# A three-block network on one core: more warming matmuls, rounded sums of squares, stacked decay terms, and another closing scaling

## Chip, cores and metric

The kernel runs on one core of one Trainium2 chip. Its time is device microseconds of one launch. The core has TensorE (PE in the rows: matmuls), VectorE (DVE), ScalarE (ACT), GpSimd (POOL) and SyncE (SP, which issues most DMAs). Each engine works through its own queue in order, and an instruction waits at the head of its queue until the semaphores of what it reads have come.

## What is computed

512 tokens of 1024 channels pass through two layers and a second block; every product is followed to float32 accuracy. Cut to what the change touches:

```python
def rms_norm(x, g):                                   # 11 places, all but one over 1024 channels or 256 of a head
    return x * rsqrt(mean(x * x, axis=-1) + EPS) * g

x = x + rglru_mixer(rms_norm(x, g_mix0)); x = x + sq_relu_mlp(rms_norm(x, g_mlp0))      # layer 0
x = x + dsa_mixer(rms_norm(x, g_mix1));   x = x + sq_relu_mlp(rms_norm(x, g_mlp1))      # layer 1
#   dsa_mixer: c = rms_norm(c, kv_norm_g) of the 128 latent channels; top-k keys by index scores; 16 heads
x = rms_norm(x, final_norm_g)                         # end of the first block ...
h = rms_norm(x, norm_mix)                             # ... and at once the first norm of the second
q, k, v, r, lr_f, lr_b, u, g_a, g_b = split(h @ w_in)
log_a_f = log_sigmoid(lr_f @ w_decay_up_fwd + b) / 16 # lr: 16 channels in each direction, decays: 512 in each
log_a_b = log_sigmoid(lr_b @ w_decay_up_bwd + b) / 16
o = gla(q, k, v, log_a_f) + gla reversed(log_a_b)     # 4 heads, o normed over 256 channels per head
x = x + merged(o, pool(u), g_a, g_b) @ w_out;  x = x + (silu(gate) * up) @ w_ffn_out
return rms_norm(x, norm_final)
```

## The kernel before

**Layout.** Activations lie channels on partitions, tokens along the row: eight tiles `xs` of 128x512. A weight chunk (128x1024, the 8 channel tiles of one output tile) is loaded by SyncE three chunks ahead, rounded by ScalarE (`wh`, L246), and GpSimd takes the exact remainder (`wl`, L247). Activations are split the same way, `split` (L350 to 355): `h` by ScalarE, L353, then `l` by VectorE, L354. Rounded numbers have the type fp32r. `group` (L339 to 342) makes a product of three passes over TensorE: wh by xh, wh by xl, wl by xh. An output tile is 24 such passes (`ps`).

**Norms.** `Feed` (L376) scales and splits the residual as it becomes ready and sums its squares tile by tile in `acc`. The norm's factor is applied behind the product: `feed.r`, asked for the first time by the evacuation of the next stage's first output tile, emits `total(acc)` (L365), one product of float32 `ones` with the sum, so that all 128 partitions hold it, and then `rsqrt_mean` (L370 to 373): square root with its table on ScalarE (`std`, L372) and reciprocal on VectorE (L373). `total` is called twelve times: for mix0, mlp0, mix1, mlp1, ffn2, the latent in `c_job` (`csq`), four GLA heads, and twice in `Feed2` (class at L980), which serves the two norms that follow one another with `acc1` and `acc`; its factor takes two reciprocals and four more steps (L993 to 1003).

**Decays.** `lr_job` evacuates the 32 low-rank channels (`lr`, L1034; the output tile holds one direction in rows 0 to 15 and the other in 32 to 47) and splits it. `decay_job`, eight times, multiplies it with one 128-column stretch of `dec`: three passes each.

**Order.** Jobs are lists of stages, and `run` (L262) emits stage n of a job n jobs behind its first; a planning scheduler then orders each engine's queue (ScalarE's by hand in the start). Before the first product of 72 passes on three output tiles (`first_products`, L511), `WARM` bfloat16 products of 128x512 run on a zero tile (L333, 334). In that start VectorE also works through a softplus of 128x8 (`sp`, L475 to 493).

**The end.** The last ffn products are made by halves of the tokens (`last_job`). `tail` norms a half: two products of `ones` with `acc2[0]` (channel tiles 0 to 6) and `acc2[1]` (tile 7), L1421, root L1425, reciprocal L1426, then `outs`: for each of 8 tiles of 128x256 either VectorE's x times gain times factor (L1435), or, for tiles 2, 3 and 7, which ScalarE has scaled by the gain (L1393), GpSimd's product with the factor (L1433); one DMA for each pair.

Of the kernel before, what the change touches and what calls it, by code (L numbers as in the profile page):

```python
# [29 lines left out]
WARM = 7  # L30
# [3 lines left out]
# the first loads in their order: input tiles, and halves of the weight chunks of the first output tiles  # L34
# [33 lines left out]
def bucket_table():  # L68
    """One-hot columns of the buckets of the distances 255, 254, ..., -127, less the last bucket's."""
    dist = 255 - np.arange(N_DIST)  # L70
    oh = np.zeros((32, DIST_PITCH), np.float32)
    oh[t5_buckets(dist), np.arange(N_DIST)] = 1.0
    oh[31, :N_DIST] -= 1.0
    return oh


def pool_edges():
    """window / count at the first and the last positions of every window."""
# [20 lines left out]
def weight_plan():  # L99
    """The key of every weight chunk in the order of use."""  # L100
# [25 lines left out]
def ktiles(w):  # L126
    """[K, N] -> [128, K / 128 * N], the K tiles side by side."""
    k, n = w.shape
    return w.reshape(k // P, P, n).transpose(1, 0, 2).reshape(P, -1)


def pack_weights(a):
    """The weights as one flat array, chunk after chunk in the order of use."""
# [4 lines left out]
    z16 = np.zeros((D, 16), np.float32)  # L138
    lr = np.concatenate([w_in2[:, 3072:3088], z16, w_in2[:, 3088:3104], np.zeros((D, 80), np.float32)], axis=1)
# [4 lines left out]
    dec[0:16, 0:512] = a["w_decay_up_fwd_2"][0]  # L144
    dec[32:48, 512:1024] = a["w_decay_up_bwd_2"][0]
# [74 lines left out]
class Weights:  # L220
    """Streams the weight chunks and splits each into a rounded part and the exact
    remainder, a number of chunks ahead of their use."""
# [39 lines left out]
def run(jobs):  # L262
    """Emits jobs in a software pipeline: stage n of a job goes out n jobs after its first stage."""
# [9 lines left out]
def build(ctx, tc, xT, wall, par, relb, onehot, edges, out):  # L273
# [50 lines left out]
    V.memset(ones, 1.0)  # L324
    ident = cp.tile([P, P], F32, name="ident")
# [4 lines left out]
    # keeps the tensor engine's clock up while the first loads come in  # L330
# [19 lines left out]
    def split(t):  # L350
        """An SBUF tile as a rounded part and the exact remainder."""
# [13 lines left out]
    def total(acc):  # L365
        ps = PS("tot")
        PE.matmul(ps, ones, acc, start=True, stop=True)
        return ps
# [7 lines left out]
    class Feed:  # L376
        """Residual tiles made ready for the next product: scaled by the norm's gain and
        split, their squares summed. The norm's own factor is applied after the product."""
# [87 lines left out]
    # softplus(-lambda); the recurrence's factors are tanh of half its logarithm, so -4 of it goes into  # L466
    # a sigmoid written as (1 + tanh) / 2
# [32 lines left out]
    def first_products():  # L500
        # the first output tiles together, in the order in which their operands come in
# [100 lines left out]
    # position bias by distance, laid out in DRAM for the diagonal reads  # L602
# [35 lines left out]
    # The queries stand in reverse order within their tiles of 128 up to the product with the values,  # L638
    # which makes the position bias of a tile a read of DRAM with two positive strides.
# [85 lines left out]
    def index_job(i, h):  # L725
        """One head's part of the index scores of query tile i."""
# [100 lines left out]
    # persistent tiles with parts that stay zero: the other head's rows of a query tile, and the  # L827
    # position bias of the keys that are further away than the last bucket's start
# [9 lines left out]
    def queries(pair, j):  # L838
        """Both heads' queries of a pair of query tiles, split, the other head's rows zero."""
# [140 lines left out]
    class Feed2(Feed):  # L980
        """The same through two norms one after the other: the first one's gain stays in the residual."""
# [44 lines left out]
    def lr_job():  # L1026
# [5 lines left out]
        def ev():  # L1032
            t = T(name="lr")
            V.tensor_mul(t, st["ps"], feed.r)  # L1034
            LR.extend(split(t))
# [3 lines left out]
    def u_job(g):  # L1039
# [5 lines left out]
        def pool():  # L1045
            # each half of the tokens with 8 more on both sides, zeros beyond the ends
            window = (2, 4, 8, 16)[g]
            st["w"] = []
            for half in range(2):
# [5 lines left out]
                while True:  # L1055
                    # new[:, i] sums the window of w around position i + lo
# [39 lines left out]
    # decays: running sums of log_sigmoid within chunks of 128, both directions  # L1096
    def decay_job(m, h):
        st = {}

        def mm():  # L1100
            if m == 0 and h == 0:
                dc.extend(W.get("dec"))
            ps = st["ps"] = PS("dec")
            o = m * 512 + h * P
            group(ps, [(dc[0][:, o:o + P], dc[1][:, o:o + P], *LR)])
# [105 lines left out]
    def gla_job(h):  # L1211
# [26 lines left out]
        def states():  # L1238
            # the state that enters each chunk, scaled to the chunk's centre
# [127 lines left out]
    feed = nxt  # L1367
    # the output's tiles by pairs of channel tiles and halves of the tokens; part of them GpSimd finishes
    pooled_out = (2, 3, 7)
    fin = {}  # L1370
    acc2 = [None, None]
# [5 lines left out]
    def final_square(d, c):  # L1377
# [5 lines left out]
        if d == 0:  # L1383
            acc2[0] = sq
        elif d < KD - 1:
            V.tensor_add(acc2[0][:, c], acc2[0][:, c], sq[:, c])
        else:
            acc2[1] = sq
        for c0 in range(c.start, c.stop, 256):
            if (d // 2, c0) not in fin:  # L1390
                fin[d // 2, c0] = T(name="fin")
            if d in pooled_out:
# [116 lines left out]
```

## Time and profile before

| | |
|---|---|
| median of 3 runs | 1916.03 us (1913.93 to 1916.14) |
| span of the profiled execution | 1913.6 us |
| TensorE busy | 1858.6 us (97%) |
| GpSimd busy | 996.1 us |
| VectorE busy | 906.4 us |
| ScalarE busy | 799.0 us |

The profiled execution's own time is not given apart from its span; the span runs from the first to the last instruction of one execution, 2.4 us under the median of the runs. A matmul's duration in the rows is modelled with its pipeline; where matmuls follow one another, the distance of their starts is what each takes from TensorE.

### The profile page before, as it was taken

The page shows a single profiled execution, that of the slowest core. Times are in us where ns is not written, and L with a number is a line of the kernel's source. Part 1 is how long each engine was busy: PE and PEld are TensorE (multiplying, and loading weights), DVE is VectorE, ACT ScalarE, POOL GpSimd, SP SyncE. Part 2 cuts the span into 40 slices and gives each one's busy share as a digit, 9 for nine tenths or more (in the row PEclk, how much of TensorE's full clock was granted, in tenths as well). Part 3 has the DMA queues.
Part 4 walks back from the last instruction along what each step waited for, and adds up shares of the span by engine and source line. Part 5 has one row for each costly group of instructions (what it writes and reads, how often), then busy time and mean ns, then how long its engine had stood idle before and what let it go on. Part 6 is the DMA issues. An engine that isn't in the chain of part 4 may idle for free.

```text
span 1913.6 us, 22395 instructions
## 1 busy us (share of the span) xinstructions
PE 1858.6 (97%) x8704; PEld 1545.4 (81%) x8704; DVE 906.4 (47%) x1170; ACT 799.0 (42%) x1248; POOL 996.1 (52%) x594
## 2 busy tenths in 40 slices
PE   8789999999999989999999999999999999999997
PEld 6567888888887778988888887888888888888886
DVE  7997440143338986543024343534466533133125
ACT  5485441233333697343124445345633333232222
POOL 5466544444563664744444457574355555455453
PEclk9999999999999999999999999999999999999999
DMA  5123222222331220233322332231123323232321
GB/s 189 66 69 99 89 98 99 99 95 93 99 110 67 80 48 18 89 100 99 99 92 96 99 100 80 90 113 61 55 78 109 100 88 101 98 100 88 100 85 58
DMA packets 53961, 172.04 MB, mean 90 GB/s; under 512 B 6288, under 2 KB 12640, under 8 KB 53856
## 3 DMA queue, kind: packets, MB, share of 16 engines
q1 hardware_dynamic: 53712, 170.62, 27.5%
q8 instruction: 68, 1.11, 0.2%
q14 instruction: 37, 0.30, 0.1%
q10 hardware_dynamic: 144, 0.00, 0.0%
HBM read 168.48 MB, written 2.12 MB: 89 GB/s over the span
## 4 chain that ended last, share of the span: by engine, by line
PE 85%; DVE 10%; ACT 3%; issue 1%; DMA 0%; POOL 0%; SPq 0%; DVEq 0%; ACTq 0%; POOLq 0%
PE ps L340 18%; PE ps L341 18%; PE ps L342 18%; PE dn L341 8%; PE dn L342 8%; PE dn L340 8%; ACT probs L889 1%; DVE score L766 1%; DVE xc L530 1%; PE o L1271 1%; DVE top L765 1%; PE ps L511 1%; PE v L1176 1%; PE v L1177 1%; PE v L1178 1%
## 5 line engine op out<-in xcount | busy, mean ns | idle before, releaser
L247 POOL TENSOR_TENSOR wl<-wst,wh 128x1024 fp32r<-128x1024 f32 (+2 forms) x314 | 755.1, 2407 | 734.0 <-ACT wh L246 715.7
L246 ACT ACTIVATE wh<-wst 128x1024 fp32r<-128x1024 f32 (+2 forms) x314 | 327.5, 1045 | 825.3 <-PE ps L341 310.3
L340 PE MATMUL ps<-xh,wh 128*128 128x512 f32 x1376 | 541.6, 394 | 8.7 <-DVE biasrow L619 5.6
L342 PE MATMUL ps<-xh,wl 128*128 128x512 f32 x1376 | 535.6, 390 | 0.0
L341 PE MATMUL ps<-xl,wh 128*128 128x512 f32 x1376 | 535.4, 389 | 0.0
L340 PEld LDWEIGHTS ps<-xh,wh 128*128 128x128 f32 x1376 | 258.8, 188 | 65.7 <-issue 8.0
L341 PEld LDWEIGHTS ps<-xl,wh 128*128 128x128 f32 x1376 | 258.8, 188 | 55.8 <-issue 2.6
L342 PEld LDWEIGHTS ps<-xh,wl 128*128 128x128 f32 x1376 | 258.6, 188 | 53.7
L340 PE MATMUL dn<-h,wh 128*128 128x512 f32 (+1 forms) x712 | 271.9, 382 | 0.0
L341 PE MATMUL dn<-l,wh 128*128 128x512 f32 (+1 forms) x712 | 271.3, 382 | 0.0
L342 PE MATMUL dn<-h,wl 128*128 128x512 f32 (+1 forms) x712 | 271.2, 382 | 0.0
L413 DVE TENSOR_TENSOR x<-x,dn 128x512 f32<-128x512 f32 x48 | 33.0, 687 | 325.3 <-PE dn L342 325.3
L340 PEld LDWEIGHTS dn<-h,wh 128*128 128x128 f32 x712 | 133.8, 188 | 26.1
L341 PEld LDWEIGHTS dn<-l,wh 128*128 128x128 f32 x712 | 133.8, 188 | 25.9
L342 PEld LDWEIGHTS dn<-h,wl 128*128 128x128 f32 x712 | 133.8, 188 | 25.7
L354 DVE TENSOR_TENSOR l<-relu,h 128x512 fp32r<-128x512 f32 x64 | 108.6, 1696 | 91.6 <-ACT h L353 91.6
L340 PE MATMUL ps<-h,wh 128*128 128x512 f32 x232 | 91.4, 400 | 12.7 <-DVE xr L525 11.1
L387 DVE SCALAR_TENSOR_TENSOR xl<-x,params,xh 128x512 fp32r<-128x512 f32 x40 | 86.3, 2161 | 27.7 <-ACT xh L386 27.7
L341 PE MATMUL ps<-l,wh 128*128 128x512 f32 x232 | 91.4, 395 | 1.6 <-DVE l L354 1.6
L342 PE MATMUL ps<-h,wl 128*128 128x512 f32 x232 | 91.1, 394 | 0.0
L444 DVE SCALAR_TENSOR_TENSOR relu<-ps,std 128x512 f32<-128x512 f32 x64 | 44.1, 690 | 86.1 <-PE ps L342 85.9
L354 DVE TENSOR_TENSOR l<-u,h 128x512 fp32r<-128x512 f32 x22 | 43.8, 1992 | 51.2 <-ACT h L353 51.2
(313 smaller groups left out, 2333.0 us busy)
## 6 DMA issues: line engine op xcount, KB each, us to landing
wst<-wall SPq DMA_DIRECT2D x300, 512.0 KB, 3.3
btile<-biasdram SPq DMA_DIRECT2D x32, 128.0 KB, 2.9
wst<-wall SPq DMA_DIRECT2D x8, 384.0 KB, 3.1
x<-xT SPq DMA_DIRECT2D x8, 256.0 KB, 5.6
out_dram<-fin SPq DMA_DIRECT2D x8, 256.0 KB, 2.5
wst<-wall SPq DMA_DIRECT2D x6, 256.0 KB, 5.7
params<-par SPq DMA_DIRECT2D x1, 76.5 KB, 4.9
oh<-onehot SPq DMA_DIRECT2D x1, 48.0 KB, 2.9
```

The lines of the kernel that those rows point to most:

```text
L246: self.nc.scalar.activation(h[:, a:b], st[:, a:b], AF.Copy)
L247: self.nc.gpsimd.tensor_sub(l[:, a:b], st[:, a:b], h[:, a:b].bitcast(F32))
L340: PE.matmul(ps, wh, xh, start=i == 0, stop=False)
L341: PE.matmul(ps, wh, xl, start=False, stop=False)
L342: PE.matmul(ps, wl, xh, start=False, stop=i == n - 1)
L354: V.tensor_sub(l, t, h.bitcast(F32))
L387: stt(l, t, g, h.bitcast(F32), op0=ALU.mult, op1=ALU.subtract)
L413: V.tensor_add(xs[j], xs[j], st["ps"])
L444: stt(t, st["ps"], 0.0, feed.r, op0=ALU.max, op1=ALU.mult)
L511: PE.matmul(first_ps[c], a[:, cols], b, start=left[c] == 3 * KD - 1, stop=left[c] == 0)
L530: stt(c[:, n:], t[:, :S - n], pc(f"conv_w{k}", j), c[:, n:], op0=ALU.mult, op1=ALU.add)
L765: V.max(top, acc[:, :w])
```

## The change

Five things, all visible in the diff below; line numbers behind L343 shift by two to eleven.

1. `WARM` goes from 7 to 17.
2. `total` splits the sum of squares (ScalarE `h`, VectorE `l`) and makes two passes with a rounded `ones_r` in place of one float32 product. All twelve callers get it.
3. The low-rank weights are stored three times (rows 0 to 31, 32 to 63, 64 to 95), the decays' weights likewise. Of the evacuated `lr`, ScalarE rounds the whole tile into `lrz`, and VectorE overwrites rows 32 to 63 with the remainder. Before the first product VectorE copies `wl` of rows 64 to 95 into `wh`. One pass over the stacked rows then holds the three terms. The loads keep their size and number.
4. At the end, ScalarE scales every tile by the gain. The squares of tiles 0 to 6 are split when tile 6 is done, the sum of a half is two rounded passes and one float32 product with tile 7's squares. `outs` is four VectorE products of 128x512 a half; GpSimd does none.
5. Comments are taken out.

```diff
-WARM = 7
+WARM = 17
...
-    lr = np.concatenate([w_in2[:, 3072:3088], z16, w_in2[:, 3088:3104], np.zeros((D, 80), np.float32)], axis=1)
+    lr = np.concatenate([w_in2[:, 3072:3104]] * 3 + [np.zeros((D, 32), np.float32)], axis=1)
...
-    dec[0:16, 0:512] = a["w_decay_up_fwd_2"][0]
-    dec[32:48, 512:1024] = a["w_decay_up_bwd_2"][0]
+    for q in range(0, 96, 32):
+        dec[q:q + 16, 0:512] = a["w_decay_up_fwd_2"][0]
+        dec[q + 16:q + 32, 512:1024] = a["w_decay_up_bwd_2"][0]
...
+    ones_r = cp.tile([P, P], F32R, name="ones_r")
+    V.tensor_copy(ones_r, ones)
...
     def total(acc):
         ps = PS("tot")
-        PE.matmul(ps, ones, acc, start=True, stop=True)
+        h, l = split(acc)
+        PE.matmul(ps, ones_r, h, start=True, stop=False)
+        PE.matmul(ps, ones_r, l, start=False, stop=True)
         return ps
...
-            t = T(name="lr")
+            t, z = T(name="lr"), T(F32R, "lrz")
             V.tensor_mul(t, st["ps"], feed.r)
-            LR.extend(split(t))
+            act(z, t, AF.Copy)
+            V.tensor_sub(z[32:64], t[32:64], z[32:64].bitcast(F32))
+            LR.append(z)
...
-                dc.extend(W.get("dec"))
+                hi, lo = W.get("dec")
+                V.tensor_copy(hi[64:96], lo[64:96].bitcast(F32))
+                dc.append(hi)
             ps = st["ps"] = PS("dec")
             o = m * 512 + h * P
-            group(ps, [(dc[0][:, o:o + P], dc[1][:, o:o + P], *LR)])
+            PE.matmul(ps, dc[0][:, o:o + P], LR[0], start=True, stop=True)
...
-            acc2[0] = sq
+            acc2.append(sq)
         elif d < KD - 1:
             V.tensor_add(acc2[0][:, c], acc2[0][:, c], sq[:, c])
+            if d == KD - 2:
+                h, l = sums[c.start] = T(F32R, "h"), T(F32R, "l")
+                act(h[:, c], acc2[0][:, c], AF.Copy)
+                V.tensor_sub(l[:, c], acc2[0][:, c], h[:, c].bitcast(F32))
         else:
-            acc2[1] = sq
+            last_sq[c.start] = sq
...
-            if d in pooled_out:
-                act(fin_half(d, slice(c0, c0 + 256)), xs[d][:, c0:c0 + 256], AF.Copy, scale=pc("g_fin2", d))
+            act(fin_half(d, slice(c0, c0 + 256)), xs[d][:, c0:c0 + 256], AF.Copy, scale=pc("g_fin2", d))
...
-            for i in range(2):
-                PE.matmul(ps, ones, acc2[i][:, c], start=i == 0, stop=i == 1)
+            h, l = sums[c.start]
+            PE.matmul(ps, ones_r, h[:, c], start=True, stop=False)
+            PE.matmul(ps, ones_r, l[:, c], start=False, stop=False)
+            PE.matmul(ps, ones, last_sq[c.start][:, c], start=False, stop=True)
...
-                for d in (2 * i, 2 * i + 1):
-                    z = fin_half(d, c)
-                    if d in pooled_out:
-                        G.tensor_mul(z, z, st["r"])
-                    else:
-                        stt(z, xs[d][:, c], pc("g_fin2", d), st["r"], op0=ALU.mult, op1=ALU.mult)
...
+                z = fin[i, c.start].rearrange("p (d c) -> p d c", d=2)
+                V.tensor_mul(z, z, st["r"].unsqueeze(1).to_broadcast([P, 2, w]))
```

The change also moves what stands around the sums in the queues. The first place is TensorE's queue at the two sums of `Feed2`, where mlp1 ends and the second block's products begin. `ps_9159` is the low-rank output tile before, `ps_9241` the last key tile ahead of the decays; `tot_9185` is the sum of `acc1`, `tot_9190` that of `acc`. Before:

```order
L342 MATMUL ps_9159<-xh_9121,wl_8991 128x512
L367 MATMUL tot_9185<-sq_8681,ones_115 128x512 [waits DVE_49]
...
L342 MATMUL ps_9159<-xh_9133,wl_8991 128x512
L367 MATMUL tot_9190<-sq_8688,ones_115 128x512 [waits Pool_49]
...
L342 MATMUL ps_9241<-xh_9133,wl_9064 128x512
L340 MATMUL dec_9274<-h_9199,wh_9154 128x512 [waits Activation_49]
L340 MATMUL dec_9280<-h_9199,wh_9154 128x512
L340 MATMUL ps_9295<-xh_8684,wh_9204 128x512
```

Now, with `tot_9223` for `acc1`, `tot_9233` for `acc`, and `ps_9287` for the second key tile, `dec` as before:

```order
L371 MATMUL tot_9223<-h_9224,ones_r_117 128x512 [waits Activation_49]
L372 MATMUL tot_9223<-l_9225,ones_r_117 128x512 [waits DVE_49]
L371 MATMUL tot_9233<-h_9234,ones_r_117 128x512 [waits Activation_49]
...
L342 MATMUL ps_9287<-xh_8721,wh_9100 128x512
...
L372 MATMUL tot_9233<-l_9235,ones_r_117 128x512 [waits DVE_49]
...
L344 MATMUL ps_9287<-xh_9170,wl_9101 128x512
L1116 MATMUL dec_9321<-lrz_9222,wh_9191 128x512 [waits DVE_49]
L1116 MATMUL dec_9325<-lrz_9222,wh_9191 128x512
```

Before, both sums stood inside the low-rank tile's 24 passes, three apart, with the 48 passes of two key tiles between the second and `dec`. Now both stand behind those 24 passes, and the second half of the second sum stands 33 passes behind its first and 15 ahead of `dec`.

The second place is VectorE's queue there. `r2` is the factor of the two norms, `k` are key tiles, `xl` the remainder of the residual's last tile. Before:

```order
L387 SCALAR_TENSOR_TENSOR xl_9134<-x_84,params_74,xh_9133 128x512 [waits Activation_49]
L373 RECIPROCAL std_9187<-std_9187 128x512 [waits Activation_49]
L998 TENSOR_TENSOR r2_9192<-tot_9190,std_9187 128x512 [waits DVE_49,PE_49]
...
L1001 RECIPROCAL r2_9192<-r2_9192 128x512 [waits Activation_49]
...
L1034 TENSOR_TENSOR lr_9184<-ps_9159,r2_9192 128x512 [waits DVE_49,Pool_49]
L354 TENSOR_TENSOR l_9200<-lr_9184,h_9199 128x512 [waits Activation_49,Pool_49]
L1141 TENSOR_TENSOR k_9266<-ps_9209,r2_9192 128x512 [waits PE_49]
L1141 TENSOR_TENSOR k_9278<-ps_9241,r2_9192 128x512 [waits PE_49,Pool_49]
```

Now:

```order
L392 SCALAR_TENSOR_TENSOR xl_9171<-x_84,params_74,xh_9170 128x512 [waits Activation_49]
L1112 CAST wh_9191<-wl_9192 32x1024 [waits Pool_49]
L356 TENSOR_TENSOR l_9225<-sq_8718,h_9224 128x512 [waits Activation_49]
L378 RECIPROCAL std_9230<-std_9230 128x512 [waits Activation_49]
L356 TENSOR_TENSOR l_9235<-sq_8725,h_9234 128x512 [waits Activation_49]
L1003 TENSOR_TENSOR r2_9240<-tot_9233,std_9230 128x512 [waits PE_49]
...
L1006 RECIPROCAL r2_9240<-r2_9240 128x512 [waits Activation_49]
...
L1041 TENSOR_TENSOR lr_9221<-ps_9196,r2_9240 128x512 [waits DVE_49]
L1152 TENSOR_TENSOR k_9312<-ps_9255,r2_9240 128x512
L1152 TENSOR_TENSOR k_9323<-ps_9287,r2_9240 128x512 [waits PE_49]
L1043 TENSOR_TENSOR lrz_9222<-lr_9221,lrz_9222 32x512 [waits Activation_49]
```

The copy of `wl` and the two remainders have come in ahead of the first step on `r2`, and the remainder of the low-rank tile, which `dec` waits for, now stands behind two key tiles. ScalarE's queue there reads `h_9224`, root of `tot_9223`, `h_9234` in this order.

The third place is ScalarE's queue at the sum of GLA head 0, behind the state updates of the next head. `state`, `en` and `cen` are that head's states and scaled keys and queries, `gb` a gate tile. Before, with `tot_10486` for the sum:

```order
L1255 ACTIVATE state_10456<-state_10456,cc_10301 128x256 [waits DVE_49]
L1291 ACTIVATE gb_10461<-gb_10461 128x512 [waits DVE_49]
L1196 ACTIVATE en_10466<-cen_10464 128x512 [waits DVE_49]
L1255 ACTIVATE state_10456<-state_10456,cc_10312 128x256 [waits DVE_49]
L1197 ACTIVATE cen_10464<-cen_10464 128x512 [waits Activation_49]
L1196 ACTIVATE en_10477<-cen_10475 128x512 [waits DVE_49,Pool_49]
...
L372 ACTIVATE std_10488<-tot_10486,eps_111 128x512 [waits PE_49]
```

Now, with `h_10518` the rounded sum that `tot_10517` waits for on TensorE, where it stands right behind the twelve `kv` passes, as `tot_10486` did:

```order
L1266 ACTIVATE state_10487<-state_10487,cc_10332 128x256 [waits DVE_49]
L1302 ACTIVATE gb_10492<-gb_10492 128x512 [waits DVE_49]
L1207 ACTIVATE en_10497<-cen_10495 128x512 [waits DVE_49]
L1266 ACTIVATE state_10487<-state_10487,cc_10343 128x256 [waits DVE_49]
L1208 ACTIVATE cen_10495<-cen_10495 128x512 [waits Activation_49]
L1207 ACTIVATE en_10508<-cen_10506 128x512 [waits DVE_49,Pool_49]
L355 ACTIVATE h_10518<-sq_10393 128x512
L1219 ACTIVATE cc_10682<-cc_10682 128x4 [waits DVE_49]
...
L377 ACTIVATE std_10524<-tot_10517,eps_111 128x512 [waits PE_49]
```

The new rounding stands behind the second `en`. Head 1 has the same order (`h_10698` behind its second `en`). At heads 2 and 3 a whole output tile of 24 passes stands ahead of the sum, now as before, and no `en` ahead of the rounding.

## Rows read from the trace of the kernel before

**Rows 1.** The profile's page: the span, the busy time of TensorE (PE) as its share of the span and its instructions, and the chain of work that ended last, by engine.

```profile
span 1913.6 us, 22395 instructions
...
PE 1858.6 (97%) x8704; PEld 1545.4 (81%) x8704; DVE 906.4 (47%) x1170; ACT 799.0 (42%) x1248; POOL 996.1 (52%) x594
...
PE 85%; DVE 10%; ACT 3%; issue 1%; DMA 0%; POOL 0%; SPq 0%; DVEq 0%; ACTq 0%; POOLq 0%
```

**Rows 2.** The view of waits for TensorE over the whole span: who waited for whom, total us, times, longest.

```profile
PE ps L340 <- DVE xr L525: 12.4, 4, 5.0
...
PE tot L367 <- ACT csq L711: 3.5, 1, 3.5
...
PE tot L1421 <- DVE sq L1386: 1.3, 1, 1.3
...
PE dec L340 <- ACT h L353: 0.6, 1, 0.6
```

**Rows 3.** The chain of work that ended last, around the sum of mlp0: start, us, what.

```profile
206.47 0.86 PE tot L367 x2
207.33 0.23 PE ps L340
```

**Rows 4.** Busy time of each engine in two stretches that follow idle time of TensorE of 4.98 and 3.45 us; the column after POOL is the granted clock of TensorE as a share of full speed.

```profile
72.60:75.60 3.00, 3.00 (x7) 2.42 (x8) 2.93 (x5) 3.00 (x6) 1.02 (x1) 0.50 0.00 0
...
612.30:614.90 2.60, 2.60 (x4) 1.43 (x5) 2.08 (x5) 0.56 (x1) 0.00 (x0) 0.50 0.45 173
```

**Rows 5.** The timeline of the start, one engine after the other: start, us, engine, line, operation, and in brackets the idle time before and what ended it.

```profile
1.25 3.09 PE L334 MATMUL warm<-warm 128*128 128x512 bf16 x7 [1.25 <-DVE eps L320]
...
8.40 0.80 PE L511 MATMUL ps<-xh,wh 128*128 128x512 f32 x1 [0.84 <-ACT wh L246]
...
14.11 0.52 PE L511 MATMUL ps<-xh,wh 128*128 128x512 f32 x1
...
25.83 2.96 ACT L246 ACTIVATE wh<-wst 128x1024 fp32r<-128x1024 f32 x3 [0.56 <-issue]
...
26.97 9.46 POOL L247 TENSOR_TENSOR wl<-wst,wh 128x1024 fp32r<-128x1024 f32 x4 [6.97 <-ACT wh L246]
...
26.11 0.69 DVE L362 TENSOR_TENSOR sq<-sq 128x512 f32<-128x512 f32 x1
...
34.02 2.44 DVE L490 TENSOR_SCALAR sp<-lam 128x8 f32<-128x8 f32 x1
...
36.85 3.35 DVE L373 RECIPROCAL std<-std 128x512 f32<-128x512 f32 x1
```

**Rows 6.** The timeline around the sum of the latent's squares (c_job).

```profile
612.23 2.08 PE L367 MATMUL tot<-csq,ones 128*128 128x512 f32 x2 [3.45 <-ACT csq L711]
...
614.34 0.69 ACT L372 ACTIVATE std<-tot,eps 128x512 f32<-128x512 f32 x1 [2.17 <-PE tot L367]
...
615.13 3.35 DVE L373 RECIPROCAL std<-std 128x512 f32<-128x512 f32 x1 [0.65 <-ACT std L372]
```

**Rows 7.** Busy time of each engine between 660 and 740 us, the first part of the attention's heads (columns as in rows 4).

```profile
660.00:740.00 80.00, 70.58 (x454) 59.95 (x455) 67.59 (x239) 71.27 (x234) 54.41 (x93) 0.98 0.22 52
```

**Rows 8.** The chain of work that ended last, from the two sums of Feed2 to the first of the decays' products.

```profile
1156.49 0.87 PE tot L367 x2
1157.39 0.70 ACT std L372
1158.11 3.36 DVE std L373
1161.57 0.70 DVE r L998
...
1169.68 0.64 ACT h L353
...
1170.36 0.73 PE dec L340 x2
```

**Rows 9.** The timeline of VectorE and GpSimd around the two sums of Feed2.

```profile
1153.20 2.48 DVE L362 TENSOR_TENSOR sq<-sq 128x512 f32<-128x512 f32 x1 [0.75 <-ACT sq L359]
...
1170.41 1.38 DVE L354 TENSOR_TENSOR l<-lr,h 128x512 fp32r<-128x512 f32 x1 [0.77 <-ACT h L353]
...
1152.72 2.41 POOL L247 TENSOR_TENSOR wl<-wst,wh 128x1024 fp32r<-128x1024 f32 x1 [2.77 <-ACT wh L246]
...
1156.02 1.45 POOL L362 TENSOR_TENSOR sq<-sq 128x512 f32<-128x512 f32 x1
```

**Rows 10.** The timeline of TensorE and ScalarE around the sums of GLA heads 0 and 1.

```profile
1321.65 1.02 PE L367 MATMUL tot<-sq,ones 128*128 128x512 f32 x2
...
1325.17 0.61 ACT L1196 ACTIVATE en<-cen 128x512 f32<-128x512 f32 x1
...
1342.96 1.02 PE L367 MATMUL tot<-sq,ones 128*128 128x512 f32 x2
...
1346.48 0.61 ACT L1196 ACTIVATE en<-cen 128x512 f32<-128x512 f32 x1
```

**Rows 11.** The chain of work that ended last, its last part.

```profile
1904.42 1.76 DVE std L1426
...
1906.21 1.05 DVE fin L1435
...
1908.12 1.65 DVE fin L1435 x3
```

More of the change, by code (lines that the diff above doesn't have):

```diff
@@ L137, in pack_weights @@
         att_in[:, 1024:1152], att_in[:, 0:1024]], axis=1)
-    z16 = np.zeros((D, 16), np.float32)
-    lr = np.concatenate([w_in2[:, 3072:3088], z16, w_in2[:, 3088:3104], np.zeros((D, 80), np.float32)], axis=1)
+    lr = np.concatenate([w_in2[:, 3072:3104]] * 3 + [np.zeros((D, 32), np.float32)], axis=1)
     first2 = {"q": 0, "k": 512, "v": 1024, "r": 2048, "u": 3104, "ga": 3616, "gb": 4640}
@@ L1367, in build @@
     feed = nxt
-    pooled_out = (2, 3, 7)
     fin = {}
-    acc2 = [None, None]
+    acc2, sums, last_sq = [], {}, {}
     def fin_half(d, c):
@@ L1429, in outs @@
             for i in pairs:
-                for d in (2 * i, 2 * i + 1):
-                    z = fin_half(d, c)
-                    if d in pooled_out:
-                        G.tensor_mul(z, z, st["r"])
-                    else:
-                        stt(z, xs[d][:, c], pc("g_fin2", d), st["r"], op0=ALU.mult, op1=ALU.mult)
-                nc.sync.dma_start(out[2 * i:2 * i + 2, :, c].rearrange("d p c -> p d c"),
-                                  fin[i, c.start].rearrange("p (d c) -> p d c", d=2))
+                z = fin[i, c.start].rearrange("p (d c) -> p d c", d=2)
+                V.tensor_mul(z, z, st["r"].unsqueeze(1).to_broadcast([P, 2, w]))
+                nc.sync.dma_start(out[2 * i:2 * i + 2, :, c].rearrange("d p c -> p d c"), z)
         return [tot, rstd, lambda: outs((1, 0)), lambda: outs((2, 3))]
```

## Prediction

> **What bounds the kernel now.** I read the page first: TensorE is busy 1858.6 of 1913.6 us and carries 85% of the chain that ended last [rows 1]. So time goes down where TensorE gets fewer passes, and up wherever it comes to wait. The view of its waits says where it waits already: in the first mixer for VectorE's xr (12.4 us), once for the latent's squares (3.5), at the first decay product only 0.6, and before the last sum 1.3 [rows 2]. Apart from the last two I found no wait of TensorE behind 760 us. There every pass saved is time saved, and every new wait is time lost, whole, unless an engine had been done before TensorE comes to the place. That is the test for each of the new steps, since the new sum of squares needs ScalarE and then VectorE before TensorE, where the old one needed neither.
>
> **What it saves on TensorE.** A float32 sum shows as two passes of together 0.86 us; the fp32r pass behind it takes 0.23 of the chain [rows 3]. Two rounded passes are then 0.45, and each of the twelve sums saves 0.41, together 4.9. The decays' eight products drop from 24 passes to 8: 16 x 0.227 = 3.6 saved, nothing hides that. The warming: seven products took 3.09, 0.44 each, and the first products of the kernel kept that half level until 14.11; from 8.40 that is thirteen of them [rows 5], each 0.21 longer than at the full level, with two before 2.9 in all.
>
> **Sums with cover.** At mlp0, mix1, mlp1 and ffn2 the sum of squares is ready several us before TensorE reaches it (the view of waits names a sum only at the latent and at the end [rows 2]), so h (0.64 [rows 8]) and l (0.7 to 2.5) are ready too: 4 x -0.41 = **-1.6**.
>
> **The start.** From 25 to 73 us the pace is VectorE's, not TensorE's. ScalarE must now round the sum, whose last addition on VectorE ends at 26.80, before the weight chunks that it began at 25.83; with 0.64 for the rounding they begin near 27.5. GpSimd's four remainders, 26.97 for 9.46 us, move by the same 1.6, and VectorE's softplus steps end only as these do (a 128x8 step took 2.44 at 34.02), so the reciprocal at 36.85 moves to about 38.1 to 38.4 [rows 5]. TensorE's 2.9 us would only lengthen its wait for xr. I take **+1**, near VectorE's shift; ends: -2.9 (TensorE's gain passes through) and +4 (three collisions more). Seventeen warming products at the half level would end at 1.25 + 17 x 0.44 = 8.7, within that.
>
> **The latent.** Today TensorE stands idle 3.45 us for csq, and runs the sum at the half level [rows 6, 4]. Now it waits 0.64 more for h; the pass with l stands 21 passes further back (4.8 us), so root and reciprocal (614.34, 615.13 [rows 6]) come about 5 later; ScalarE and VectorE have other work behind them, and by the queue VectorE does four to five more rounds of the key selection before the heads. The heads start some 8 later. From 660 to 740 VectorE is busy 67.6 and ScalarE 71.3 of 80 us, TensorE 70.6 [rows 7], so part is regained and part not: I take **+4**, ends 0 and +8.
>
> **Feed2, the dearest place.** Today the chain runs from the two sums through 12.5 us on ScalarE and VectorE to the first decay product at 1170.36 [rows 8], and TensorE has work for all but 0.56 of it [rows 2]: no slack. Three things lengthen it. (a) The first remainder needs VectorE, where the new copy waits for GpSimd: VectorE's square sum took 2.48 beside GpSimd's split of 2.41, and GpSimd's square sum runs to 1157.47 [rows 9]. Copy and remainder end near 1159.0, TensorE is there three passes behind 1156.49, at 1157.2: idle 1.9. (b) The second h stands on ScalarE behind the root of the first sum: 0.70 + 0.64 [rows 8], idle 1.4. (c) The second remainder's pass stands 33 passes (7.5 us) behind its h, 15 before dec. The h pass starts at about 1160.7, so the sum is complete near 1168.6; it was complete at 1157.36 + 0.68 + 0.86 = 1158.9, and r, which began at 1161.57 behind the first reciprocal, now begins near 1168.9. From r to the end of the low-rank rounding takes 1170.32 - 1161.57 = 8.75 [rows 8]: 1177.7. Two key tiles and the remainder of rows 32 to 63 follow on VectorE, 0.7 each free, 1.4 to 2.5 beside GpSimd [rows 9]: dec at 1179.0 to 1181.5. TensorE ends its 15 passes at 1172 and is idle 7 to 9.5 us. Idle of 4.98 and 3.45 us let its clock fall to 0.50 for some 3 us afterwards [rows 4], 1.4 lost. The sum: 1179.0 or 1181.5 against 1170.36, 9.9 in the middle, with the clock and both sums' saving in it: **+11.5**, ends +9 and +17 (every VectorE step there stalled). Behind it **-3.6** for the decays' passes.
>
> The Trainium skill (SBUF — State Buffer, section "SBUF: two separate sides") says that VectorE and GpSimd share one pair of ports, held by whoever starts first for the whole instruction. The 2.48 us at 1153.20 agree; that rule alone would put every added VectorE step beside a GpSimd split at the end of the split, the upper end above.
>
> **GLA heads 0 and 1.** The old sum ran at 1321.65 and 1342.96, right behind kv, with no wait [rows 10]. The new h stands on ScalarE behind the second en, which starts at 1325.17 and 1346.48 and takes 0.61 [rows 10]; with 0.64 for h it is ready at 1326.35 and 1347.7. TensorE waits 4.7 each time, 9.4, and each wait is as long as the ones behind which the clock was 0.50 [rows 4]: 2 x 1.4. At heads 2 and 3 a tile of 24 passes stands in between, and h is ready. Less 4 x 0.41: **+10.6**, ends +7 (no fall of the clock) and +12.5.
>
> **The end.** Behind the last reciprocal VectorE's share was 1.05 + 0.86 + 1.65 = 3.56 [rows 11]; four products of 128x512 at 0.7 make 2.8. Before it a rounded pass more and fewer steps of VectorE in the way: **-0.5**, ends -1.2 and +0.8. If the eight DMAs pace the end, the gain is gone.
>
> **Sum.** 1 - 1.6 + 4 + 11.5 - 3.6 + 10.6 - 0.5 = +21.4 us, a span of 1935.0. The median of the runs is 2.4 over the span, and stays so: 1916.0 + 21.4 = **1937.4 us**.
>
> **Rivals.**
> - *Only TensorE's work counts* (the other sign): h and l are ready everywhere. -4.9 - 3.6 - 2.9 - 0.5 = -11.9: 1904.1. It decides by one thing: whether ScalarE ends h before TensorE ends kv and the low-rank tile. For it speaks that ten of twelve sums of squares are complete long before; against it that ScalarE's queue is in order and en and the first root stand ahead. 0.09.
> - *One of the two stalls is covered.* If ScalarE reaches h before en's inputs come, the heads give -1.6 instead of 10.6: 1925.2. If Feed2's r comes in time, that term is 3.3 - 0.8 instead of 11.5: 1928.4. The queues speak against both. 0.17.
> - *VectorE loses to GpSimd at each added step*: five steps (one at the start, one at the latent, three at Feed2) at 2.48 - 0.69 = 1.8: +9, 1946.4. The row at 1153.20 speaks for it; that GpSimd is busy half the time [rows 1] against five of five. 0.12.
> - *Half and half*: gains as in the first rival and one stall of about 12 cancel: 1912.2 to 1919.9. 0.07.
>
> **Numbers.** The forecast, both stalls in full, 1931 to 1944, has 0.55. The range 1919 to 1948 takes in the forecast, the covered stall and most of the collisions, and leaves out about 2 in 10. This kernel's measurement tells apart some 0.2% (3.8 us): faster 0.09, the same 0.07, slower 0.84.
>
> **What would show it.** In TensorE's waits: tot for ScalarE's h with three or more entries, two of them 4 to 5 us, the latent's 4.1; dec for VectorE's lrz with 7 us or more; tot for VectorE's l of 1 to 2. A granted clock of 0.50 for some 3 us behind each of the three long ones. TensorE's first products 0.23 apart instead of 0.43, and the first reciprocal on VectorE still no earlier than 36.85. Eight dec passes, 0.23 apart. The heads' begin some 8 us later. Wrong would be: h on ScalarE before the second en, or r at Feed2 before 1165, or stalls at sums that I called covered.

## The result

The changed kernel takes 1939.2 us (median of 4 runs, 1938.4 to 1941.1) against 1915.6 of the kernel before (4 runs, 1913.9 to 1916.1): a ratio of 1.012, 95% interval 1.0108 to 1.0132. It is slower by 23.7 us; 1937.4 was forecast, with 1919 to 1948 as the range. The profiled execution's span is 1939.3 us, against 1913.6 [rows 1]. From its page, the span and the busy time of TensorE:

```profile
span 1939.3 us, 22396 instructions
...
PE 1865.7 (96%) x8698; PEld 1550.6 (80%) x8698; DVE 909.3 (47%) x1184; ACT 811.2 (42%) x1272; POOL 990.4 (51%) x588
```

TensorE has six instructions less and is busy 7.1 us longer: the warming adds 3.6 (6.73 us for 3.09 [rows 5]), the shorter sums and decays take some away, and more of its passes run at half the clock (the mean granted clock is 0.984, 0.991 before). The other 18.6 of the 25.7 us are idle time. The view of waits for TensorE in the changed kernel (who waited for whom, total us, times, longest):

```profile
PE tot L371 <- ACT h L355: 14.5, 4, 4.6
PE ps L342 <- DVE xr L530: 10.9, 3, 5.0
PE dec L1116 <- DVE lrz L1043: 6.1, 1, 6.1
...
PE ps L342 <- DVE qq L785: 4.3, 2, 4.1
...
PE ps L342 <- ACT dots L743: 2.7, 2, 2.5
PE tot L1434 <- ACT h L1399: 2.3, 1, 2.3
...
PE tot L372 <- DVE l L356: 1.5, 1, 1.5
```

Against [rows 2] four large lines are new or grown: the sums' wait for h (14.5, where the one for csq was 3.5), the decays' wait for lrz (6.1, where the one for h was 0.6), and two in the attention that no part of the change names, qq and dots. Two small ones are the last sum's (2.3 for 1.3) and the one for a remainder (1.5).

**Feed2.** The timeline there, TensorE first, then VectorE, ScalarE and GpSimd (it answers to [rows 8, 9]; by then everything stands 6.2 us later, which is what the latent cost less what was won ahead of it):

```profile
1165.13 0.49 PE L372 MATMUL tot<-l,ones_r 128*128 128x512 f32 x1 [1.49 <-DVE l L356]
1166.92 0.50 PE L371 MATMUL tot<-h,ones_r 128*128 128x512 f32 x1 [1.30 <-ACT h L355]
1176.36 0.40 PE L372 MATMUL tot<-l,ones_r 128*128 128x512 f32 x1
1186.26 1.22 PE L1116 MATMUL dec<-lrz,wh 128*128 128x512 f32 x2 [6.11 <-DVE lrz L1043]
...
1162.60 1.75 DVE L1112 CAST wh<-wl 32x1024 fp32r<-32x1024 f32 x1
...
1169.65 0.63 DVE L356 TENSOR_TENSOR l<-sq,h 128x512 fp32r<-128x512 f32 x1
1176.79 0.69 DVE L1003 TENSOR_TENSOR r<-tot,std 128x512 f32<-128x512 f32 x1 [6.51 <-PE tot L372]
...
1166.25 0.62 ACT L355 ACTIVATE h<-sq 128x512 fp32r<-128x512 f32 x1
...
1162.25 1.47 POOL L364 TENSOR_TENSOR sq<-sq 128x512 f32<-128x512 f32 x1
```

Read it from dec backwards. dec waited 6.11 us for lrz. VectorE's step r, with which the way to lrz begins, had itself been idle 6.51 us for the second remainder's pass, and that pass had nothing to wait for, since its remainder l was ready at 1170.28: it merely stood 33 passes back in TensorE's queue. TensorE kept VectorE waiting, and 10 us later VectorE kept TensorE waiting.

**The heads.** The timeline of TensorE and ScalarE at head 0, against [rows 10]:

```profile
1333.83 2.75 PE L1256 MATMUL kv<-v,keT 128*128 128x256 f32 x12
1341.12 0.50 PE L371 MATMUL tot<-h,ones_r 128*128 128x512 f32 x1 [4.54 <-ACT h L355]
...
1345.04 0.46 PE L342 MATMUL ps<-xh,wh 128*128 128x512 f32 x1
...
1339.93 0.61 ACT L1207 ACTIVATE en<-cen 128x512 f32<-128x512 f32 x1
1340.45 0.61 ACT L355 ACTIVATE h<-sq 128x512 fp32r<-128x512 f32 x1
```

h runs at once behind the second en. Its sum of squares had been complete long before, as an experiment below shows. Behind the wait TensorE's clock falls; busy time in two stretches there, the granted clock behind POOL's column (0.51 is the half level, 1.2 GHz, in nearly the whole stretch):

```profile
1341.10:1342.00 0.90, 0.88 (x3) 0.76 (x4) 0.90 (x2) 0.58 (x2) 0.90 (x2) 0.86 0.00 0
1342.10:1345.20 3.10, 3.10 (x9) 2.43 (x8) 2.75 (x4) 1.49 (x2) 1.53 (x1) 0.51 0.00 0
```

**The latent.** The timeline of TensorE, ScalarE and VectorE, against [rows 6]:

```profile
625.76 0.50 PE L342 MATMUL ps<-xh,wh 128*128 128x512 f32 x1 [2.50 <-ACT dots L743]
651.69 0.50 PE L342 MATMUL ps<-h,wh 128*128 128x512 f32 x1 [4.06 <-DVE qq L785]
...
618.54 0.69 ACT L377 ACTIVATE std<-tot,eps 128x512 f32<-128x512 f32 x1 [7.12 <-PE tot L372]
...
619.26 3.35 DVE L378 RECIPROCAL std<-std 128x512 f32<-128x512 f32 x1 [1.32 <-ACT std L377]
```

ScalarE's root stood 7.12 us at the head of its queue; behind it are the index scores (dots) whose output tiles TensorE needs free. The reciprocal begins 4.1 us later than before.

**The start.** The timeline of ScalarE, GpSimd and VectorE, against [rows 5]:

```profile
26.81 0.63 ACT L355 ACTIVATE h<-sq 128x512 fp32r<-128x512 f32 x1 [1.56 <-DVE sq L364]
27.35 3.89 ACT L246 ACTIVATE wh<-wst 128x1024 fp32r<-128x1024 f32 x4
...
28.48 12.02 POOL L247 TENSOR_TENSOR wl<-wst,wh 128x1024 fp32r<-128x1024 f32 x5 [8.51 <-ACT wh L246]
...
28.56 2.35 DVE L496 TENSOR_TENSOR sp<-sp,sp 128x8 f32<-128x8 f32 x1
...
33.27 3.35 DVE L378 RECIPROCAL std<-std 128x512 f32<-128x512 f32 x1
```

The reciprocal starts 3.6 us earlier than at 36.85, not later.

### The profile page after: what moved, and what is told of

The parts are those of the page before. It is cut to its first block, busy times and chain, and to the rows that moved or that the text cites. A ratio compares the mean times of both kernels' runs of the same rounds, so it can differ in the third digit from the quotient of the medians.

```text
span 1939.3 us, 22396 instructions
## 1 busy us (share of the span) xinstructions
PE 1865.7 (96%) x8698; PEld 1550.6 (80%) x8698; DVE 909.3 (47%) x1184; ACT 811.2 (42%) x1272; POOL 990.4 (51%) x588
## 4 chain that ended last, share of the span: by engine, by line
PE 59%; ACT 2%; DVE 2%; issue 0%; DVEq 0%; POOL 0%; ACTq 0%
PE ps L344 13%; PE ps L342 13%; PE ps L343 13%; PE dn L342 5%; PE dn L343 5%; PE dn L344 5%; PE o L1282 1%; PE v L1187 1%; PE v L1189 1%; PE v L1188 1%; ACT probs L894 1%; PE kv L1256 0%; PE s L1237 0%; ACT pTh L914 0%; PE pT L911 0%
## 5 line engine op out<-in xcount | busy, mean ns | idle before, releaser
L343 PE MATMUL ps<-xl,wh 128*128 128x512 f32 x1376 | 538.3, 392 | 0.0
L343 PEld LDWEIGHTS ps<-xl,wh 128*128 128x128 f32 x1376 | 260.7, 189 | 54.6
L343 PE MATMUL dn<-l,wh 128*128 128x512 f32 (+1 forms) x712 | 271.3, 382 | 0.0
L343 PEld LDWEIGHTS dn<-l,wh 128*128 128x128 f32 x712 | 133.8, 188 | 26.1
L342 PEld LDWEIGHTS dn<-h,wh 128*128 128x128 f32 x712 | 133.8, 188 | 25.7
L343 PE MATMUL ps<-l,wh 128*128 128x512 f32 x232 | 92.8, 401 | 1.4 <-DVE l L356 1.4
L342 PEld LDWEIGHTS ps<-h,wh 128*128 128x128 f32 x232 | 45.0, 194 | 29.4 <-DVE xr L530 10.3
```

The lines of the kernel that those rows point to most:

```text
L342: PE.matmul(ps, wh, xh, start=i == 0, stop=False)
L343: PE.matmul(ps, wh, xl, start=False, stop=False)
```

## The experiments

All ratios are to the kernel before, run on the same chip. The changed kernel was not run again beside the experiments, so a difference from it is one of ratios, or of medians taken at different times. Besides the medians, one table goes through all of it: the time between landmarks on TensorE in each profiled execution (the start of the sums of mlp0, mix1, mlp1 and ffn2, the first kv pass of the group in front of head 0's sum, and the end of the span).

| kernel | to mlp0 | mix1 to mlp1 | mlp1 to kv | kv to ffn2 | ffn2 to end | ratio (95%) |
|---|---|---|---|---|---|---|
| before | 206.3 | 258.1 | 505.7 | 241.9 | 352.6 | 1 |
| changed | 205.1 | 266.3 | 513.8 | 253.3 | 352.2 | 1.0120 (1.0108 to 1.0132) |
| split sums alone | 206.6 | 264.4 | 515.7 | 253.3 | 352.2 | 1.0133 (1.0117 to 1.0148) |
| warming alone | 207.7 | 259.1 | 505.7 | 241.9 | 352.7 | 0.9997 (0.9989 to 1.0006) |
| stacked decays alone | 206.0 | 259.4 | 503.5 | 241.9 | 352.6 | 0.9990 (0.9981 to 0.9999) |
| closing scaling alone | 205.3 | 259.4 | 505.7 | 241.9 | 352.1 | 0.9998 (0.9989 to 1.0007) |
| heads split early | 205.1 | 266.3 | 513.8 | 240.3 | 351.8 | 1.0053 (1.0038 to 1.0068) |
| latent float32 | 203.0 | 258.5 | 514.9 | 252.9 | 351.7 | 1.0094 (1.0078 to 1.0111) |
| Feed2 float32 | 204.9 | 266.0 | 503.1 | 253.7 | 352.2 | 1.0065 (1.0050 to 1.0080) |
| wait filled | 204.2 | 266.0 | 513.7 | 250.1 | 352.2 | 1.0109 (1.0094 to 1.0124) |
| three repairs | 203.6 | 258.6 | 503.1 | 240.3 | 352.2 | 0.9964 (0.9950 to 0.9978) |
| Feed2 split early | 203.8 | 258.7 | 511.6 | 240.3 | 351.7 | 1.0003 (0.9994 to 1.0012) |

From mlp0 to mix1 it is 349.0 with float32 sums and 348.7 with rounded ones, throughout.

### Each part alone

The split sums alone, on the kernel before (`ones_r` as in the diff of the change):

```diff
-        PE.matmul(ps, ones, acc, start=True, stop=True)
+        h, l = split(acc)
+        PE.matmul(ps, ones_r, h, start=True, stop=False)
+        PE.matmul(ps, ones_r, l, start=False, stop=True)
```

> The kernel before with the split sums alone (all twelve). Theory (the split's waits are the loss, in three places): latent and heads +8, Feed2 +10, GLA heads 0 and 1 +11, sums with cover -1.5: about +28 us. Rival (the loss at the latent and the heads comes from another order of the queues that any of the five parts sets off, and the one at Feed2 from the stacked decays): +12 or less, only the two GLA waits of 4.6 us with their clock.

1943.2 us (4 runs) against 1916.4: +26.8. The three stretches grow by 6.3, 10.0 and 11.4 us. So the split sums are the whole loss and more; the rival is out. At Feed2 they alone make dec wait, without any stacked term:

```profile
1183.73 1.22 PE L342 MATMUL dec<-h,wh 128*128 128x512 f32 x2 [4.80 <-ACT h L355]
```

The warming alone:

```diff
-WARM = 7
+WARM = 17
```

> The kernel before with seventeen warming products alone. Theory (VectorE sets the pace from 25 to 73 us): TensorE ends its first 72 passes 2.8 us earlier and waits longer for xr; of that -1 to -1.5 us arrives at the first sum of mlp0. Rival one (TensorE's gain passes through): -2.9. Rival two (the planner orders the attention otherwise as soon as anything ahead changes, and that is the latent's loss): +5 to +8, between 600 and 820 us.

1916.1 us (11 runs) against 1916.4; the interval, -2.1 to +1.1, holds zero and also the -1 to -1.5 of the theory, so the runs don't decide between these. TensorE's first sum starts at 29.5 where it was 32.6, and in this trace none of that is left at mlp0 (207.7 against 206.3). Rival one, -2.9, is outside the interval; rival two is out too, for between mix1 and mlp1 this kernel takes 259.1, like the two below.

The stacked decays alone (weights, `lr_job` and `decay_job` as in the diff of the change):

```diff
-            group(ps, [(dc[0][:, o:o + P], dc[1][:, o:o + P], *LR)])
+            PE.matmul(ps, dc[0][:, o:o + P], LR[0], start=True, stop=True)
```

> The kernel before with the stacked decay terms alone. Theory: sixteen passes less, -3.6; the first decay product waits for two key tiles and the remainder of 32 rows on VectorE, +1 to +2.2: -1.4 to -2.6 us in all. Rival (the stacked decays are the loss at Feed2): +3 to +6, with a wait of several us for lrz.

1914.5 us (11 runs) against 1916.4, -1.9; from mlp1 to kv -2.2. The first product waits 2.03 us:

```profile
1172.87 0.73 PE L1109 MATMUL dec<-lrz,wh 128*128 128x512 f32 x2 [2.03 <-DVE lrz L1036]
```

Saved passes 3.6, wait 1.5 longer than the 0.56 of before: 2.1, where the trace shows 2.2 and the medians 1.9. The rival is out.

The closing scaling alone (`final_square`, `tail` and what they use, as in the diff of the change):

```diff
-                        stt(z, xs[d][:, c], pc("g_fin2", d), st["r"], op0=ALU.mult, op1=ALU.mult)
+                V.tensor_mul(z, z, st["r"].unsqueeze(1).to_broadcast([P, 2, w]))
```

> The kernel before with the new closing scaling alone. Theory: -0.5 to +0.3 us, a shorter VectorE end against a new wait of the last sum for h (2.3 us in place of 1.3). Rival (GpSimd's products had been free and VectorE now does all): +1 to +2.

1916.2 us (11 runs) against 1916.4. Its last stretch is 0.5 us shorter in the trace; the median can't tell that (its interval is -2.1 to +1.3), and it is the trace alone that speaks against the rival. In the changed kernel the last sum waits 2.29 us for h where it waited 1.33 for sq, and the four closing products take 2.50 us where the chain had 3.56 [rows 11]:

```profile
1928.88 0.58 PE L1434 MATMUL tot<-h,ones_r 128*128 128x256 f32 x1 [2.29 <-ACT h L1399]
...
1933.23 2.50 DVE L1446 TENSOR_TENSOR fin<-fin,std 128x512 f32<-128x512 f32 x4
```

The four parts come to 26.8 - 0.2 - 1.9 - 0.2 = +24.5, the whole change to +23.7: within the uncertainty of the runs they add.

### Each of the three places undone

The heads' sums split where they are made, in the changed kernel (`total` takes the two parts where it is given them):

```diff
-            st["acc"] = acc
+            st["hl"] = split(acc)          # in outputs
...
-            o_rstd[h] = rsqrt_mean(total(st["acc"]), 256)
+            o_rstd[h] = rsqrt_mean(total(None, st["hl"]), 256)
```

> The changed kernel with the heads' sums of squares split where they are made (in outputs) and not where the sum is taken (in norm), so that ScalarE's rounding stands ahead of the next head's en. Theory (the 4.6 us at heads 0 and 1 are ScalarE's queue): both waits gone and the clock stays at 1.00 there, from kv of head 0 to the sum of ffn2 11.4 + 1.6 = 13 us less than before the edit at most, about -12 against the changed kernel: 1927. Rival (the rounding or the two passes cost by themselves): -4 or less.

1927.2 us (4 runs): -12 against the changed kernel, and kv to ffn2 falls to 240.3, 1.6 under the kernel before, which is four times the 0.41 that a sum saves. Two lines of its timeline, ScalarE's h and TensorE's sum:

```profile
1327.52 0.63 ACT L355 ACTIVATE h<-sq 128x512 fp32r<-128x512 f32 x1 [0.24 <-DVE sq L364]
```

```profile
1336.24 0.58 PE L371 MATMUL tot<-h,ones_r 128*128 128x512 f32 x1
```

The sum of squares was complete at 1327.5; the same rounding that ended at 1341.06 ends at 1328.2, and TensorE does not wait. So the wait came of the place in ScalarE's queue: the rounding and the two passes are the same.

What of it was the clock, the next kernel tells. Sixteen products that nobody reads stand in the wait:

```diff
+            if h < 2:
+                w = PS("warm")
+                for _ in range(16):
+                    PE.matmul(w, warm[:, :P], warm, start=True, stop=True)
             o_rstd[h] = rsqrt_mean(total(st["acc"]), 256)
```

> The changed kernel with sixteen bfloat16 products of 128x512 on the zero tile ahead of the sums of heads 0 and 1 (3.5 us each, inside the wait of 4.6; they compute nothing that is used). Theory (part of the loss there is the clock's fall behind the wait): the waits stay as long counted from kv's end, the granted clock stays at 1.00: -2.5 to -3 us against the changed kernel. Rival (the wait is all): 0 to +1.

1937.2 us (4 runs); kv to ffn2 is 250.1, 3.2 less than in the changed kernel; the ratio, 1.0109 against 1.0120, points the same way, but the intervals overlap. TensorE reaches the sum 3.5 us later and starts it at the same distance from kv (7.29 us both times); the stretch behind it has the full clock:

```profile
1339.92 0.50 PE L371 MATMUL tot<-h,ones_r 128*128 128x512 f32 x1 [1.09 <-ACT h L355]
```

```profile
1339.90:1342.80 2.90, 2.88 (x13) 2.38 (x14) 2.90 (x4) 0.87 (x4) 2.54 (x2) 1.00 0.00 0
```

By the trace the clock's fall costs 1.6 us behind each wait; the medians are 2.0 us apart.

The float32 sum for the latent alone, in the changed kernel (`total32` is the old `total`):

```diff
-            st["r"] = rsqrt_mean(total(st["sq"]), P)
+            st["r"] = rsqrt_mean(total32(st["sq"]), P)
```

> The changed kernel with the old float32 sum for the latent alone. Theory (the latent's later factor holds up ScalarE's and VectorE's queues, and TensorE with them): the waits for dots (2.5) and qq (4.1) go back to nothing and 0.8, the heads begin as early as before: -6 to -7.5 us, 1932. Rival (the attention comes out otherwise ordered by the other parts): within 2 us of the changed kernel.

1934.7 us (4 runs), some 5 us less than the changed kernel by the ratios, where 6 to 7.5 were expected. The stretch from mix1 to mlp1 goes back by 7.8 to 258.5, and the long waits for qq and dots are gone (0.2 is left for dots): theory right there. The profiled execution, 1931.5, is 3.2 under the median, so the trace flatters this kernel elsewhere, at the start above all (203.0). But 1.1 came back at Feed2, which the edit doesn't touch. VectorE's two multiplications of r fell beside GpSimd's work, which fell differently in the changed kernel (0.70 and 1.06 there):

```profile
1167.64 1.90 DVE L1009 TENSOR_TENSOR r<-r,std 128x512 f32<-128x512 f32 x1
...
1173.72 2.12 DVE L1012 TENSOR_TENSOR r<-r,std 128x512 f32<-128x512 f32 x1
```

```profile
1178.52 1.22 PE L1121 MATMUL dec<-lrz,wh 128*128 128x512 f32 x2 [8.24 <-DVE lrz L1048]
```

The float32 sums in Feed2 alone, in the changed kernel:

```diff
-                self.r1 = rsqrt_mean(total(self.acc1), D)
-                ps = total(self.acc)
+                self.r1 = rsqrt_mean(total32(self.acc1), D)
+                ps = total32(self.acc)
```

> The changed kernel with the old float32 sums in Feed2 alone. Theory (the second sum's late second pass delays r by 7 us): the wait for lrz falls from 6.1 to the 2.0 us that the stacked decays show alone, the waits for h and l go: -9 to -11 us, 1929. Rival (VectorE's copy and remainder for the stacked decays do it): -3 or less.

1929.1 us (4 runs), -10; mlp1 to kv is 503.1, 10.7 less than in the changed kernel, and dec waits the 2.03 us of the stacked decays alone:

```profile
1177.67 0.73 PE L1121 MATMUL dec<-lrz,wh 128*128 128x512 f32 x2 [2.03 <-DVE lrz L1048]
```

So the loss here is the split sums' and not that of the copy and the remainder for the decays. As both sums changed whole, this doesn't show how much of it is the late pass.

### Repairs together

All three repairs in one kernel (heads split early, float32 at the latent and in Feed2; everything else as changed):

> The changed kernel with all three repairs: heads' sums split where they are made, float32 sums at the latent and in Feed2. Theory (the three places are the whole loss, and they add): what is left of the change is eight rounded sums with cover (8 x -0.41 = -3.3), the stacked decays (-2) and the end (-0.4): about -5.5 us against the kernel before, 1911, faster than both. Rival (the repairs overlap, or the savings of the covered sums don't arrive): within 2 us of the kernel before.

1910.2 us (5 runs, 1907.6 to 1911.7) against 1917.1: 0.9964, interval 0.9950 to 0.9978. It beats both kernels by more than the uncertainty. Every stretch is where its own experiment had put it. Its waits keep one line of the change's at Feed2:

```profile
PE tot L377 <- ACT csq L721: 3.5, 1, 3.5
...
PE dec L1121 <- DVE lrz L1048: 2.0, 1, 2.0
```

Can Feed2 keep the rounded sums, if the split is written ahead of the evacuation that asks for the factor? In the kernel with the three repairs (`r` then takes `hl1` and `hl`):

```diff
+            if len(self.X) == KD - 1:
+                self.hl1 = split(self.acc1)
             act(t, t, AF.Copy, scale=pc(self.g1, len(self.X)))
             super().add(t)
+            if len(self.X) == KD:
+                self.hl = split(self.acc)
```

> As the kernel with all three repairs, but Feed2 keeps the rounded sums and splits them as soon as its last tile is added, ahead of the evacuation that asks for the factor; the second remainder's pass then stands 21 passes behind its h, 33 before. Theory (it is the late pass that delays r): r about 5 us behind the first sum, some 1.5 us later than with float32 sums; wait for lrz 3 to 4 us, 0.8 saved by the passes: +0.5 to +2 against the three repairs, and 7 us or more better than the same without the early split. Rival (the two roundings on ScalarE and VectorE delay it as such): +6 or more against the three repairs.

1916.9 us (11 runs) against 1917.1: 6.6 more than the three repairs. Here my theory was wrong and the rival right. Its timeline at Feed2, TensorE, VectorE and GpSimd:

```profile
1158.98 0.80 PE L371 MATMUL tot<-h,ones_r 128*128 128x512 f32 x1 [1.49 <-ACT h L355]
1165.56 0.40 PE L372 MATMUL tot<-l,ones_r 128*128 128x512 f32 x1
1176.23 1.22 PE L1125 MATMUL dec<-lrz,wh 128*128 128x512 f32 x2 [4.15 <-DVE lrz L1052]
```

```profile
1158.96 2.45 DVE L356 TENSOR_TENSOR l<-sq,h 128x512 fp32r<-128x512 f32 x1 [2.25 <-ACT h L355]
...
1161.33 3.34 DVE L383 RECIPROCAL std<-std 128x512 f32<-128x512 f32 x1
```

```profile
1158.48 2.37 POOL L247 TENSOR_TENSOR wl<-wst,wh 128x1024 fp32r<-128x1024 f32 x1 [2.33 <-ACT wh L246]
```

The second remainder lost 1.8 us to GpSimd's split and stood ahead of the first reciprocal; TensorE waited 1.49 for the second h and once more, 1.67, for the residual's last remainder, which VectorE now takes behind the new steps. r began at 1165.99, where the three repairs have it at 1158.6, and only 1.33 us of that was a wait for the late pass. So the late pass was only one of several delays; each step that Feed2 gets on ScalarE or VectorE lies on its way to dec.

## Why the prediction was right, step by step

Direction, cause and size were right: 1937.4 against 1939.2. That the sum came so near is in part luck: the start was 2.2 us better than forecast and hid half of what the latent cost more. By its own terms, from the table above:

| term | forecast | measured |
|---|---|---|
| start | +1 | -1.2 in this pair of traces, not told from zero |
| four sums with cover | -1.6 | -1.6 (0.4 at mlp0 and at ffn2, taken over for mix1 and mlp1) |
| latent and heads | +4 | +8.6 (266.3 - 258.1, and mix1's own 0.4) |
| Feed2 and decays | +11.5 - 3.6 = +7.9 | +8.5 (513.8 - 505.7, and mlp1's own 0.4) |
| GLA heads | +10.6 | +11.4 |
| end | -0.5 | 0.0 (352.2 - 352.6, and ffn2's own 0.4) |
| sum | +21.4 | +25.7 in the spans, +23.7 in the medians |

**GLA.** The mechanism was right and shown by undoing it: 4.54 and 4.60 where 4.7 was forecast. The clock was priced at 1.4 for each wait and measured 1.6.

**Feed2.** The steps came in the order of the forecast: idle for the first remainder 1.49 (1.9), for the second h 1.30 (1.4), r held until the late pass, dec 6.11, under its 7 to 9.5. Counted without the 6.2 us, dec starts at 1180.1, inside 1179.0 to 1181.5, but two errors cancel there. I priced the clock at 1.4, once, behind dec; it was at the half level twice:

```profile
1167.80:1171.00 3.20, 3.20 (x9) 2.52 (x8) 2.48 (x2) 0.00 (x0) 1.19 (x1) 0.50 0.50 164
...
1186.30:1191.40 5.10, 5.10 (x12) 4.08 (x13) 0.00 (x0) 4.28 (x7) 0.00 (x0) 0.50 0.32 103
```

The first stretch follows the two short waits, lies ahead of the late pass, and r came 1.7 later than I had it (1170.6 for 1168.9). From r to dec it then took 9.5 us, not 10.1 to 12.6. By the distance of the starts, 0.43 where 0.23 is usual, I estimate 1.6 us for the first stretch and 2.6 for the second. The term's own sum is also off: 9.9 and 1.4 make 11.3, not 11.5.

**VectorE beside GpSimd.** The copy of wl took 1.75 and ended at 1164.35, behind GpSimd's square sum that ended at 1163.72. The Trainium skill (SBUF — State Buffer, section "SBUF: two separate sides") has GpSimd and a VectorE operation with two inputs in SBUF, or in a mode that takes both ports, share a pair of ports that whoever starts first holds for the whole instruction. This copy (0.68 us in the last experiment, where it started ahead of GpSimd's square sum) and the 2.45 us remainder above agree with it. The upper end of the range, every step stalled, did not come; the latent's repair shows two stalls of it.

**The latent: the term that was mis-sized.** The mechanism was named (root and reciprocal about 5 later, work of ScalarE and VectorE behind them, the heads some 8 later) and is shown by undoing it: from the sum of mix1 to the heads' first logit product it is 98.7 us before, 106.6 in the changed kernel, 98.8 with the float32 sum. That is 7.9 for the 8. But I took 4 of 8 as regained between 660 and 740 because TensorE, VectorE and ScalarE have some 10 us free there [rows 7]. They regained nothing: from the heads' first to their last logit product 90.3 us pass before and 90.5 after, 90.5 too with the float32 sum. Free time inside a chain in which each engine waits for the next was no slack here. Part of the 8.6 is the reference: three kernels whose attention is untouched take 259.1 to 259.4 from mix1 to mlp1, the profiled one of before 258.1; counted from those three the term is 7.3 to 7.6.

**The start: the step that failed.** I let GpSimd's remainders move by 1.6 us, as they did (28.48 for 26.97, 1.5 us), and had VectorE's softplus move with them. It was the other way: VectorE gained the time before GpSimd began, did most of its small steps free, and met GpSimd at two of them instead of four; the reciprocal came 3.6 us earlier. Hardly anything of it reaches mlp0. The twelve traces reach that sum between 203.0 and 207.7, and those with both the split and 17 warming products are the early ones (203.0 to 205.1); the parts alone are not. With one trace of each I leave it open whether the pair gives some 2 us. That the warming alone doesn't give the 2.9 us that TensorE saves is measured.

**The end.** Alone, the closing scaling gives the 0.5 in its trace; in the changed kernel it is gone, and by the traces the clock takes it. In the changed kernel the granted clock is 0.50 from the last sum on and ffn2 to end takes 352.2; with the heads split early it is still 1.00 over that sum, and the same code takes 351.8. The other five traces of this ending fall into the same two groups: 352.2 in three with 0.50 over that sum, 351.7 in two where the clock falls behind it.

**The stacked decays** were right in size. That the decays' saving stayed small because lrz stands behind two key tiles was right too: 2.03 us.

**The rivals.** "Only TensorE's work counts" fell at the point named: ScalarE ends h 4.5 us after TensorE ends kv. Its price, -11.9, is more than even the three repairs gave (-6.8), which leave out three of its sums. "One stall covered" did not happen, but the repairs of one place came out close to its prices: 1927.2 for 1925.2, 1929.1 for 1928.4. "VectorE loses at each step" happened at single steps.

## What to carry to other kernels

A cheaper product is only cheaper if its operands are ready when TensorE's queue reaches it: ask of each new step on another engine what stands ahead of it in that engine's queue, not how long it takes. Steps that only wait for data known early belong where the data is made, not where the result is asked for. A product of two passes with work between them delivers at the second, so what reads it waits for the later place in the queue; and idle time on an engine inside a ring of waits should not be counted as slack: here none of it was.

## What the runs showed of the hardware

- The clock can fall after the wait is over. At head 0 TensorE waited 4.54 us, then ran its first 0.9 us with a mean granted clock of 0.86 and only from 1342.1 to 1345.2 at 0.51, the half level (1.2 GHz), while it was fully busy. Behind idle time of 4.98 us before, it was at 0.50 at once [rows 4].
- The clock also fell behind two short waits: at Feed2 TensorE stood 1.49 and 1.30 us with one pass between them, and from 1167.8 to 1171.0 the granted clock was 0.50.
- Filling such a wait with sixteen unused products kept the clock at 1.00 and, in the trace, took 3.2 us off for two waits.
- The start varies by some 2 us among executions of kernels with the same start (203.0 to 205.1 for the sum of mlp0 in seven traces), most of the 2.9 us that the warming could at most have given.
